# A decoder trunk in split fp32: v projected from the transposed, unscaled x, the MLP's square on ScalarE, and the order of three matmuls

## The chip, the core and the metric

The kernel runs on one core of a Trainium2 chip. The metric is the device time of one execution in microseconds. Of the kernel before there are three timed runs and one profiled execution. TensorE (PE in the profile) multiplies, ScalarE (ACT), VectorE (DVE) and GpSimd (POOL) do the elementwise work, and SyncE (SP) issues nearly all the DMA transfers. Sums of matmuls are gathered in eight PSUM banks of 128 partitions by 512 fp32 numbers.

## The reference

512 tokens of 1024 numbers go through two layers. Layer 0 mixes with a forgetting attention of 16 heads, layer 1 with a short convolution; each mixer is followed by an MLP with a squared ReLU and by a gated embedding.

```python
def rmsnorm(x, g):
    return x * lax.rsqrt(jnp.mean(x * x, -1, keepdims=True) + 1e-6) * g

def fox_attention(h, w_in, b_f, w_out):         # h: 512 x 1024, 16 heads of 64
    proj = h @ w_in                             # q, k, v and 16 forget logits
    ...
    c = lax.cumsum(log_sigmoid(f_logit + b_f))  # over the tokens
    s = q @ k.T / 8 + c[:, None] - c[None, :]   # causal, softmax, times v
    return o @ w_out

def sq_relu_mlp(h, w_up, w_down):               # 1024 -> 4096 -> 1024
    return jnp.square(jax.nn.relu(h @ w_up)) @ w_down

for i in range(2):
    m = fox_attention(rmsnorm(x, g[0]), ...) if i == 0 else short_conv(...)
    x = x + rmsnorm(m, g[1])
    x = x + rmsnorm(sq_relu_mlp(rmsnorm(x, g[2]), ...), g[3])
    x = x + rmsnorm((p[i] @ w_ple_proj[i]) * sigmoid(rmsnorm(x, g[4]) @ w_ple_gate[i]), g[5])
```

## The kernel before, in words

**Numbers.** Each fp32 operand of a matmul is held as a pair of fp32r tiles, a high part and a low part. `split` (L231 to L234) makes a pair: a cast on ScalarE writes the high part, a subtraction on VectorE (for some weights GpSimd) the low part. `mm3` (L223) multiplies two pairs with three matmuls: high by high, low of the first operand by high of the second, high of the first by low of the second. The profile names them L225, L226 and L227. Weights arrive by DMA in one of 14 raw buffers (`raw`) and are split into `wh` and `wl`; `prepare` emits these splits a number of tiles ahead.

**The start.** x is loaded by token blocks of 128 (`xa`, `xc`). The gain of the first norm is spread over the partitions by two matmuls with a row of ones (L883, `g`). For each token block, ScalarE sums squares (`junk`, L256), GpSimd makes the reciprocal root (`n_r_y`), VectorE multiplies x by root and gain (`n_h`, L264), TensorE transposes in eight 128 by 128 pieces (`n_p`, L273), and the result is split into `hTh` and `hTl` by `keep`. From hT the kernel projects v in three column chunks: chunk 0 (272 columns: 256 of v and the 16 forget logits), chunk 1 (512) and chunk 2 (256), each for one token block after the other and all eight k inside a block. `keep_v` splits the sums of v from PSUM into pages (L233 and L234, two pieces of 128 by 128 for each 256 columns). `logs` makes log-sigmoids, `tri` is a triangle of ones (L620), and `sums_of_logs` multiplies them on TensorE (`ps_c`, L388) into the running sum c. c goes to DRAM as `neg_c` and comes back as a bias of the scores. Then come the q and k projections (`qk`), the scores (`sc`), softmax and `ps_o`.

**The MLP.** FF is worked in eight groups. `up` multiplies and hands a bank to a ReLU on ScalarE (`r`, L731), then VectorE squares it (`q`, L717). In the first seven groups the down product is done in seven products on half-size blocks, with sums of blocks of q made on GpSimd (`s`, L745); the pieces of q and their sums are split into `A11h`, `A11l`, `A12h`, `A12l`, `S1h` and so on by `split`. The last group makes the square twice: once on ScalarE straight into the high part (`hh`, L807) and once on VectorE (`q`), so that the low part (`hl`, L810) is the difference. The first group of an MLP is done in two halves of 256 tokens.

**What sets the order.** Inside `manual_schedule` blocks the engines run in program order. Elsewhere a scheduler places the instructions of each engine by its own simulation of the program. Each engine then runs its own queue in order; a DMA queue issues in order, with at most eight transfers of SP's under way. The manual block of the start ends with the splits of v's chunk 0; `tri`, `logs` and what follows are placed by the scheduler.

Of the kernel before, what the change touches and what calls it, by code (L numbers as in the profile page):

```python
# [41 lines left out]
LATE = 0  # L42
PLE_OFF = 34000
# [22 lines left out]
def trunk(ctx: ExitStack, tc, g4T, x, pT, g, wv, wqk, bf, wo, wci, cw, wco, wup, wdn, wpp, wpg, out):  # L66
# [156 lines left out]
    def mm3(ps, a, b, start, stop):  # L223

        nc.tensor.matmul(ps, a.hi, b.hi, start=start, stop=False)  # L225
        nc.tensor.matmul(ps, a.lo, b.hi, start=False, stop=False)  # L226
        nc.tensor.matmul(ps, a.hi, b.lo, start=False, stop=stop)  # L227
        streamed[0] += 3 * ps.shape[-1]
        due()

    def split(hi, lo, src, eng=nc.vector):  # L231

        nc.scalar.copy(hi, src)  # L233
        eng.tensor_tensor(out=lo, in0=src, in1=hi.bitcast(F32), op=ALU.subtract)  # L234

# [82 lines left out]
    def load_x(name, t):  # L318
        xs = [page(f"{name}{t}_{n}") for n in range(2)]
        for n in range(2):  # L320
            eng = nc.scalar if name == "xa" and n else nc.sync
            eng.dma_start(xs[n][:, :S], x[t * P : (t + 1) * P, n * S : (n + 1) * S])
# [30 lines left out]
    def attention(hT, first_x, g0, by_hand):  # L353
# [49 lines left out]
        def values(c, t, soon=SOON, between=None):  # L403

            c0, width = V_CHUNKS[c]
            n_v = min(width, D - c0)
            ps = bank(f"v{c}_{t}")
            for k in range(KT):
                if width == 256:
                    w = wide("v", c, k // 2).at(lambda u: u[:, k % 2 * 256 : k % 2 * 256 + 256])  # L410
                else:
                    w = wide("v", c, k, soon=soon)
                if k == 5 and between:
                    between()
                mm3(ps[:, :width], tokens(hT, k, t), w, k == 0, k == KT - 1)

            def keep_v():
# [12 lines left out]

            return keep_v
# [150 lines left out]
        name = "n0"  # L582
        E, done_v = mybir.EngineType, []
# [410 lines left out]
```

## Time and the profile before

| | us |
|---|---|
| three timed runs | 1247.27, 1247.38, 1251.42 |
| their median | 1247.38 |
| the profiled execution's own time | 1249.03 |
| span of the profile, first to last instruction | 1247.3 |
| TensorE busy | 1222.8 |
| VectorE busy | 909.4 |
| ScalarE busy | 626.1 |
| GpSimd busy | 639.4 |

The granted TensorE clock was 0.997 of full speed over the span. Durations of matmuls overlap in the profile, since the next one starts before the last one's results are out: for how long TensorE is held by a matmul, one reads the distance from its start to the next start. The waits view sums, for each pair of instructions, how long an engine stood still for the other. The timeline lists an engine's instructions with their start, with the idle time ahead of them in brackets.

### The profile page before, as it was taken

The page shows a single profiled execution, that of the slowest core. Times are in us where ns is not written, and L with a number is a line of the kernel's source. Part 1 is how long each engine was busy: PE and PEld are TensorE (multiplying, and loading weights), DVE is VectorE, ACT ScalarE, POOL GpSimd, SP SyncE. Part 2 cuts the span into 40 slices and gives each one's busy share as a digit, 9 for nine tenths or more (in the row PEclk, how much of TensorE's full clock was granted, in tenths as well). Part 3 has the DMA queues.
Part 4 walks back from the last instruction along what each step waited for, and adds up shares of the span by engine and source line. Part 5 has one row for each costly group of instructions (what it writes and reads, how often), then busy time and mean ns, then how long its engine had stood idle before and what let it go on. Part 6 is the DMA issues. An engine that isn't in the chain of part 4 may idle for free.

```text
span 1247.3 us, 17921 instructions
## 1 busy us (share of the span) xinstructions
PE 1222.8 (98%) x5972; PEld 1024.7 (82%) x5972; DVE 909.4 (73%) x1386; ACT 626.1 (50%) x1325; POOL 639.4 (51%) x647
## 2 busy tenths in 40 slices
PE   7999999999999999999999999999999999999997
PEld 5888887788888888887889988889778888888785
DVE  5657787676888878979867444457778898779962
ACT  5467787555544534454655233333654345525541
POOL 2028766147878777875311000017777778778210
PEclk9999999999999999999999999999999999999999
DMA  7455442541343224427513232432422442236401
GB/s 254 150 139 157 127 123 65 160 145 56 123 135 100 77 95 135 128 68 255 142 51 106 75 96 87 162 118 69 127 62 82 136 135 93 68 110 184 137 17 52
DMA packets 82943, 143.45 MB, mean 115 GB/s; under 512 B 9825, under 2 KB 17041, under 8 KB 82849
## 3 DMA queue, kind: packets, MB, share of 16 engines
q1 hardware_dynamic: 82640, 142.03, 37.3%
q8 instruction: 47, 0.77, 0.3%
q14 instruction: 48, 0.39, 0.1%
q10 hardware_dynamic: 144, 0.26, 0.1%
q0 software_dynamic: 64, 0.00, 0.0%
HBM read 135.89 MB, written 6.37 MB: 114 GB/s over the span
## 4 chain that ended last, share of the span: by engine, by line
PE 74%; DVE 10%; POOL 5%; issue 4%; ACT 3%; DMA 3%; SPq 0%; DVEq 0%; POOLq 0%; ACTq 0%
PE dn L226 6%; PE dn L227 5%; PE up L226 5%; PE up L225 5%; PE up L227 5%; PE dn L225 5%; DVE wl L234 5%; POOL s L745 3%; PE pg L227 2%; PE pg L225 2%; PE pg L226 2%; PE qk L225 2%; PE qk L226 2%; PE qk L227 2%; DVE acc L777 2%
## 5 line engine op out<-in xcount | busy, mean ns | idle before, releaser
L234 DVE TENSOR_TENSOR wl<-raw,wh 128x512 fp32r<-128x512 f32 (+1 forms) x372 | 345.8, 979 | 27.0 <-ACT wh L233 26.7
L226 PE MATMUL up<-hTh,wl 128*128 128x512 f32 (+1 forms) x576 | 210.2, 365 | 0.0
L227 PE MATMUL up<-hTl,wh 128*128 128x512 f32 (+1 forms) x576 | 209.7, 366 | 0.0
L225 PE MATMUL up<-hTh,wh 128*128 128x512 f32 (+1 forms) x576 | 209.3, 366 | 0.0
L233 ACT CAST wh<-raw 128x512 fp32r<-128x512 f32 (+1 forms) x372 | 202.1, 619 | 1.9 <-PE ps_o L534 1.6
L234 POOL TENSOR_TENSOR wl<-T,wh 128x512 fp32r<-128x512 f32 x112 | 160.5, 1466 | 35.8 <-ACT wh L233 32.0
L225 PEld LDWEIGHTS up<-hTh,wh 128*128 128x128 f32 x576 | 108.6, 189 | 17.5
L226 PEld LDWEIGHTS up<-hTh,wl 128*128 128x128 f32 x576 | 108.6, 189 | 17.5
L227 PEld LDWEIGHTS up<-hTl,wh 128*128 128x128 f32 x576 | 108.3, 189 | 17.5
L777 DVE TENSOR_TENSOR acc<-dn,acc 128x512 f32<-128x512 f32 x168 | 107.3, 678 | 9.5 <-PE dn L227 9.4
L134 POOL TENSOR_TENSOR T<-raw,raw 128x512 f32<-128x512 f32 x56 | 88.7, 1596 | 36.9 <-DMA raw<-in_wdn 28.9
L731 ACT ACTIVATE r<-up 128x512 f32<-128x512 f32 (+1 forms) x72 | 38.7, 547 | 125.5 <-PE up L227 116.6
L134 POOL TENSOR_TENSOR T<-raw,T 128x512 f32<-128x512 f32 x56 | 91.4, 1632 | 2.2
L717 DVE TENSOR_TENSOR q<-r 128x512 f32<-128x512 f32 (+1 forms) x72 | 68.1, 952 | 29.0 <-ACT r L731 28.9
L248 POOL TENSOR_SCALAR cor_r_v<-cos,cos 128x1 f32<-128x1 f32 x4 | 1.6, 396 | 159.1 <-ACT junk L256 159.1
L233 ACT CAST A11h<-q 128x256 fp32r<-128x256 f32 x28 | 11.4, 406 | 100.7 <-DVE q L717 100.7
L233 ACT CAST wh<-T 128x512 fp32r<-128x512 f32 x112 | 61.2, 617 | 0.0
L784 POOL TENSOR_TENSOR acc<-acc,acc 128x512 f32<-128x512 f32 x28 | 46.9, 1707 | 10.0 <-DVE acc L777 10.0
L225 PE MATMUL qk<-hTh,wh 128*128 128x512 f32 x128 | 50.8, 397 | 0.0
L227 PE MATMUL qk<-hTl,wh 128*128 128x512 f32 x128 | 50.4, 394 | 0.0
L226 PE MATMUL qk<-hTh,wl 128*128 128x512 f32 x128 | 50.4, 393 | 0.0
L225 PE MATMUL pg<-wh,hTh 128*128 128x512 f32 x128 | 50.3, 393 | 0.0
(240 smaller groups left out, 3133.3 us busy)
## 6 DMA issues: line engine op xcount, KB each, us to landing
raw<-in_wup SPq DMA_DIRECT2D x128, 256.0 KB, 2.9
raw<-in_wdn SPq DMA_DIRECT2D x128, 256.0 KB, 2.8
raw<-in_wci SPq DMA_DIRECT2D x48, 256.0 KB, 3.0
raw<-in_wqk SPq DMA_DIRECT2D x32, 256.0 KB, 3.3
raw<-in_wpg SPq DMA_DIRECT2D x32, 256.0 KB, 3.6
g<-in_g SPq DMA_DIRECT2D x18, 256.0 KB, 5.7
prl<-neg_c SPq DMA_DIRECT2D x16, 256.0 KB, 6.6
raw<-in_wo SPq DMA_DIRECT2D x16, 256.0 KB, 2.8
```

Of the source, the lines that this page charges most:

```text
L134: nc.gpsimd.tensor_tensor(out=B[name, p], in0=B[a, p], in1=B[b, p], op=ALU.subtract)
L225: nc.tensor.matmul(ps, a.hi, b.hi, start=start, stop=False)
L226: nc.tensor.matmul(ps, a.lo, b.hi, start=False, stop=False)
L227: nc.tensor.matmul(ps, a.hi, b.lo, start=False, stop=stop)
L233: nc.scalar.copy(hi, src)
L234: eng.tensor_tensor(out=lo, in0=src, in1=hi.bitcast(F32), op=ALU.subtract)
L248: nc.gpsimd.tensor_scalar(out=v, in0=parts[0], scalar1=parts[1], scalar2=EPS, op0=ALU.add, op1=ALU.add)
L717: nc.vector.tensor_tensor(out=out, in0=r, in1=r, op=ALU.mult)
L731: nc.scalar.activation(r[:, :n], ps[:, :n], AF.Relu)
L745: sums = lambda out, a, b, op: nc.gpsimd.tensor_tensor(out=out, in0=a, in1=b, op=op)
L777: nc.vector.tensor_tensor(out=a, in0=banks[s], in1=a, op=ALU.add)
L784: nc.gpsimd.tensor_tensor(out=a, in0=a, in1=acc[i, s][:, :S], op=ALU.add)
```

## The change

The host hands over two more arrays: `xT`, which is x transposed (eight tiles of 128 features by 512 tokens), and `g0T`, the gain of the first norm as a column for each tile. Four things follow.

1. The start no longer transposes. `uT[k]` is xT[k] times its gain, split by `split_by` (ScalarE, then one VectorE instruction); v is projected from uT, and each token's root `r0[t]` is multiplied in when v is split from PSUM. Chunks 0 and 1 now run k outside and the four token blocks inside, so each holds four banks. For q and k, the roots are spread as a row over all partitions by four matmuls (`r_row`), and `normed_tokens(k)` multiplies xT[k] by gain and row (`h`) and splits that into `hTh` and `hTl`. The manual block now reaches to the splits of v's chunk 1 and the first four `normed_tokens`.
2. Before the first projection TensorE does sixteen matmuls of 128 by 128 on a tile of zeros (`warm`, `idle`).
3. `square` in the MLP runs on ScalarE.
4. `mm3` does high by high, high by low, low by high.

```diff
         nc.tensor.matmul(ps, a.hi, b.hi, start=start, stop=False)
-        nc.tensor.matmul(ps, a.lo, b.hi, start=False, stop=False)
-        nc.tensor.matmul(ps, a.hi, b.lo, start=False, stop=stop)
+        nc.tensor.matmul(ps, a.hi, b.lo, start=False, stop=False)
+        nc.tensor.matmul(ps, a.lo, b.hi, start=False, stop=stop)
...
+    def split_by(hi, lo, src, by):
+
+        nc.scalar.mul(hi, src, by)
+        nc.vector.scalar_tensor_tensor(
+            out=lo, in0=src, scalar=by, in1=hi.bitcast(F32), op0=ALU.mult, op1=ALU.subtract
+        )
...
-        vs = [[page(f"v{t}_{i}", F32R) for i in range(4)] for t in range(NB)]
+        vs = [{} for _ in range(NB)]
...
-        def values(c, t, soon=SOON, between=None):
+        def keep_v(c, t, ps):
...
             n_v = min(width, D - c0)
+            if n_v < width:
+                nc.vector.scalar_tensor_tensor(
+                    out=logit[:, t * H : (t + 1) * H], in0=ps[:, n_v:width], scalar=r0[t],
+                    in1=b_f, op0=ALU.mult, op1=ALU.add,
+                )
+            for c1 in range(0, n_v, 256):
+                src = ps[:, c1 : c1 + 256].rearrange("p (h d) -> p h d", d=HD)
+                b = (c0 + c1) // 256
+                vs[t][b] = page(f"v{t}_{b}", F32R)
+                block = vs[t][b].rearrange("p (h r) -> p h r", r=P)
+                split_by(block[:, :, :HD], block[:, :, HD:], src, r0[t])
+
+        def values(c, t):
+
-                if n_v < width:
-                    nc.vector.tensor_tensor(
-                        out=logit[:, t * H : (t + 1) * H], in0=ps[:, n_v:width], in1=b_f,
-                        op=ALU.add,
-                    )
-                for c1 in range(0, n_v, 256):
-                    src = ps[:, c1 : c1 + 256].rearrange("p (i e d) -> p i e d", e=2, d=HD)
-                    block = vs[t][(c0 + c1) // 256].rearrange("p (i r) -> p i r", i=2)
-                    for e in range(2):
-                        hi = block[:, :, 192 * e : 192 * e + HD]
-                        lo = block[:, :, 64 + 64 * e : 128 + 64 * e]
-                        split(hi, lo, src[:, :, e, :])
-
-            return keep_v
+                w = wide("v", c, k // 2).at(lambda u: u[:, k % 2 * 256 : k % 2 * 256 + 256])
+                mm3(ps[:, :256], tokens_of(uT[k], t), w, k == 0, k == KT - 1)
+            keep_v(c, t, ps)
...
-        def rows(t):
-            r = stats(t, first_x[t], name)
-            return [scaled(t, n, first_x[t], r, g0, name) for n in range(2)]
-
-        def turn_rows(t, hs):
-            for n in range(2):
-                keep(t, n, turned(t, n, hs[n], name), hT)
+        E = mybir.EngineType
+        r0, uT = {}, []
+        r_row, every = page("r_row"), page("every")
+        nc.gpsimd.memset(every[:, :P], 1.0)
+
+        def chunk(c, after):
+
+            width = V_CHUNKS[c][1]
+            banks = [bank(f"v{c}_{t}") for t in range(NB)]
+            for k in range(KT):
+                if c == 0:
+                    uT.append(Pair(page(f"uTh{k}", F32R), page(f"uTl{k}", F32R)))
+                    split_by(uT[k].hi[:, :S], uT[k].lo[:, :S], first_xT[k][:, :S], g0_col[:, k : k + 1])
+                w = wide("v", c, k, soon=0)
+                for t in range(NB):
+                    mm3(banks[t][:, :width], tokens_of(uT[k], t), w, k == 0, k == KT - 1)
+                after(k)
+            return banks
...
         with tc.manual_schedule(engines={E.PE, E.DVE, E.Activation}):
-            r = stats(0, first_x[0], name)
-            prepare(3)
-            hs = {0: [scaled(0, n, first_x[0], r, g0, name) for n in range(2)]}
-            prepare(4)
-            for n in range(2):
-                keep(0, n, turned(0, n, hs[0][n], name), hT)
-                prepare(5 + n)
-            prepare(KT)
-            hs[1] = rows(1)
-            hs[2] = rows(2)
+            banks = {0: chunk(0, lambda k: None)}
+
+            def between(k):
+                t = k - 1
+                if 0 <= t < NB:
+                    r0[t] = stats(t, first_x[t], "n0")
+                    nc.gpsimd.tensor_scalar(
+                        out=every[:, (t + 1) * P : (t + 2) * P] if t < NB - 1 else diag[:, :P],
+                        in0=ident, scalar1=r0[t], scalar2=None, op0=ALU.mult,
+                    )
+                if k >= NB:
+                    keep_v(0, k - NB, banks[0][k - NB])
+                    prepare(where["v", 2, 0] + 1 + k - NB)
+
+                if k == KT - 2:
+                    spread = bank("r_row")
+                    for t in range(NB):
+                        nc.tensor.matmul(
+                            spread[:, t * P : (t + 1) * P], every[:, :P],
+                            every[:, (t + 1) * P : (t + 2) * P] if t < NB - 1 else diag[:, :P],
+                            start=True, stop=True,
+                        )
+                    nc.scalar.copy(r_row[:, :S], spread)
+
+            def normed_tokens(k):
+                h = page(f"h0_{k}")
+                nc.vector.scalar_tensor_tensor(
+                    out=h[:, :S], in0=first_xT[k][:, :S], scalar=g0_col[:, k : k + 1],
+                    in1=r_row[:, :S], op0=ALU.mult, op1=ALU.mult,
+                )
+                split(hT.hi[:, k, :], hT.lo[:, k, :], h[:, :S])
+
+            diag = page("diag")
+            banks[1] = chunk(1, between)
+            prepare(where["qk", 0, 0] + 2)
             for t in range(NB):
-                between = (lambda: turn_rows(t + 1, hs[t + 1])) if t + 1 < NB else None
-                done_v.append(values(0, t, 0, between))
-                if t + 3 < NB:
-                    hs[t + 3] = rows(t + 3)
-                if t:
-                    prepare(KT + 3 * t)
-                    done_v.pop(0)()
-        done_v.pop(0)()
+                keep_v(1, t, banks[1][t])
+                normed_tokens(t)
         tri = page("tri", F32R)
         ones = page("ones")
...
         nc.vector.tensor_copy(tri[:, :S], ones[:, :S])
         logs()
         for t in range(NB):
-            values(1, t)()
-            if t == 2:
+            values(2, t)
+            normed_tokens(NB + t)
+            if t == 1:
                 sums_of_logs(tri)
         bias(0)
         bias(1)
-        for t in range(NB):
-            values(2, t)()
...
         def square(out, r):
-            nc.vector.tensor_tensor(out=out, in0=r, in1=r, op=ALU.mult)
+            nc.scalar.activation(out, r, AF.Square)
...
+        nc.scalar.dma_start(g0_col, g0T)
+        for k in range(KT):
+            (nc.scalar if k < 2 else nc.sync).dma_start(first_xT[k][:, :S], xT[k])
+            fetch(k + 1)
+        first_x = []
+        for t in range(NB):
+            fetch(KT + t + 1)
+            first_x.append(load_x("xc", t))
+    idle = bank("idle")
+    for _ in range(WARM):
+        nc.tensor.matmul(idle[:, :P], warm[:, :P], warm[:, :P], start=True, stop=True)
```

The order of the instructions moves at three places. The first is VectorE's queue in the start, around the making of `tri`. Before, it stood among the small steps of the logs (`f_u`, `f_r`, `f_ru`), after the last split of v's chunk 0 (`v_3`):

```order
L369 TENSOR_SCALAR f_u<-f_e 128x64
L234 TENSOR_TENSOR v_3_147<-v_3_412,v_3_147 128x2x64
L372 SCALAR_TENSOR_TENSOR f_r<-f_u,f_e 128x64
L620 CAST tri<-ones 128x512
L375 RECIPROCAL f_ru<-f_u 128x64
```

Now it stands behind the splits of chunk 1 of all four token blocks and behind four `normed_tokens`; these are the last rows of that chain, for token block 3 and k of 3, with the preceding block's end:

```order
L629 SCALAR_TENSOR_TENSOR h_2_602<-xT_90,g_col,r_row 128x512
L235 TENSOR_TENSOR hTl<-h_2_602,hTh 128x512
L240 SCALAR_TENSOR_TENSOR v_0_606<-v_3_345,n_r_y,v_0_606 128x4x64
L240 SCALAR_TENSOR_TENSOR v_1_609<-v_3_345,n_r_y,v_1_609 128x4x64
L629 SCALAR_TENSOR_TENSOR h_3_612<-xT_91,g_col,r_row 128x512
L648 CAST tri<-ones 128x512
L235 TENSOR_TENSOR hTl<-h_3_612,hTh 128x512
```

The splits of v wait for ScalarE and, through it, for TensorE, and `hTl` waits for ScalarE's `hTh`. `tri` needs only GpSimd's triangle of ones, but it is made after them, since the queue runs in order.

The second place is TensorE's queue where it uses `tri`. Before, `ps_c` followed the third token block of v's chunk 1 (512 columns):

```order
L225 MATMUL v_2_598<-wh_443,hTh 128x512
L226 MATMUL v_2_598<-wh_443,hTl 128x512
L227 MATMUL v_2_598<-wl_444,hTh 128x512
L388 MATMUL ps_c<-tri,lf_h 16x512
L388 MATMUL ps_c<-tri,lf_l 16x512
L388 MATMUL ps_c<-tri,lf_h 16x384
```

Now it follows the second token block of chunk 2 (256 columns), and the other two token blocks of chunk 2 come behind it:

```order
L226 MATMUL v_1_709<-wh_558,uTh_321 128x256
L227 MATMUL v_1_709<-wl_559,uTh_321 128x256
L228 MATMUL v_1_709<-wh_558,uTl_322 128x256
L395 MATMUL ps_c<-tri,lf_h 16x512
L395 MATMUL ps_c<-tri,lf_l 16x512
L395 MATMUL ps_c<-tri,lf_h 16x384
```

The first row of `ps_c` waits for the cast of `tri` on VectorE, and all of TensorE's work behind it waits with it.

The third place is ScalarE's queue in the first group of the MLP (names carry layer, group, f and half). Before, ReLUs stood next to each other and the squares on VectorE:

```order
L731 ACTIVATE r_0_0_256_3931<-up_0_0_256_3906 128x256
L731 ACTIVATE r_0_1_256_3961<-up_0_1_256_3936 128x256
L233 CAST A12h_0_1_3964<-q_0_1_3691 128x512
L233 CAST S1h_0_1_3972<-s_0_1_3968 128x512
L233 CAST S3h_0_1_3976<-s_0_0_3934 128x512
```

Now each ReLU is followed by its square, and what VectorE held of these rows is gone there:

```order
L758 ACTIVATE r_0_0_256_3932<-up_0_0_256_3907 128x256
L744 ACTIVATE q_0_0_3691<-r_0_0_256_3932 128x256
L758 ACTIVATE r_0_1_256_3962<-up_0_1_256_3937 128x256
L744 ACTIVATE q_0_1_3692<-r_0_1_256_3962 128x256
L234 CAST A12h_0_1_3965<-q_0_1_3692 128x512
L234 CAST S1h_0_1_3973<-s_0_1_3969 128x512
L234 CAST S3h_0_1_3977<-s_0_0_3935 128x512
```

Here `A12h` needs the square on its own engine alone, where before it waited for another engine; the casts behind it keep their order.

More of the change, by code (lines that the diff above doesn't have):

```diff
@@ L42 @@
 LATE = 0
+WARM = 16
 PLE_OFF = 34000
@@ L65, in trunk @@
 @with_exitstack
-def trunk(ctx: ExitStack, tc, g4T, x, pT, g, wv, wqk, bf, wo, wci, cw, wco, wup, wdn, wpp, wpg, out):
+def trunk(ctx: ExitStack, tc, g4T, x, xT, pT, g, g0T, wv, wqk, bf, wo, wci, cw, wco, wup, wdn, wpp, wpg, out):
     nc = tc.nc
@@ L320, in load_x @@
         for n in range(2):
-            eng = nc.scalar if name == "xa" and n else nc.sync
-            eng.dma_start(xs[n][:, :S], x[t * P : (t + 1) * P, n * S : (n + 1) * S])
+            nc.sync.dma_start(xs[n][:, :S], x[t * P : (t + 1) * P, n * S : (n + 1) * S])
         return xs
@@ L351, in mixer_out, with attention @@
                 then(t)
-    def attention(hT, first_x, g0, by_hand):
+    def attention(hT, first_xT, g0_col, first_x, by_hand):
         b_f = consts.tile([P, H], F32, tag="bf", name="b_f")
-        vs = [[page(f"v{t}_{i}", F32R) for i in range(4)] for t in range(NB)]
+        vs = [{} for _ in range(NB)]
         n_f = NB * H
@@ L867, in ple @@
                 then(t)
-    one = page("one")
-    nc.vector.memset(one[:1, :P], 1.0)
-    rows = [page(f"row{n}") for n in range(2)]
-    for n in range(2):
-        nc.gpsimd.dma_start(rows[n][:1, :], g[0:1, n * S : (n + 1) * S])
-    with tc.manual_schedule(engines={mybir.EngineType.SP, mybir.EngineType.Activation}):
-        first_x = [load_x("xa", 0)]
-        fetch(4)
-        first_x.append(load_x("xc", 1))
-        fetch(KT)
-        first_x += [load_x("xc", t) for t in (2, 3)]
-    g0 = [bank(f"g0_{n}") for n in range(2)]
-    for n in range(2):
-        nc.tensor.matmul(g0[n], one[:1, :P], rows[n][:1, :], start=True, stop=True)
+    g0_col = consts.tile([P, KT], F32, tag="g0_col", name="g0_col")
+    warm = page("warm")
+    nc.vector.memset(warm[:, :S], 0.0)
+    first_xT = [page(f"xT{k}") for k in range(KT)]
+    with tc.manual_schedule(engines={mybir.EngineType.SP, mybir.EngineType.Activation}):
+        nc.scalar.dma_start(g0_col, g0T)
[9 more added lines that the diff above has]
+        nc.tensor.matmul(idle[:, :P], warm[:, :P], warm[:, :P], start=True, stop=True)
     kept = dram.tile([2, NB, 2, P, S], F32, tag="kept", name="kept")
@@ L886, in trunk @@
     by_hand = ExitStack()
-    lhs, opened = attention(hT, first_x, g0, by_hand)
+    lhs, opened = attention(hT, first_xT, g0_col, first_x, by_hand)
     oT = lhs
```

12 lines of the change are left out of this document (2 added, 10 removed).

## The prediction, on record before the kernel ran

> **What bounds the kernel now.** First the page's busy times, and GpSimd's busy tenths in forty slices of 31 us:
>
> ```profile
> PE 1222.8 (98%) x5972; PEld 1024.7 (82%) x5972; DVE 909.4 (73%) x1386; ACT 626.1 (50%) x1325; POOL 639.4 (51%) x647
> POOL 2028766147878777875311000017777778778210
> ```
>
> TensorE bounds it: time can only come from where TensorE stands still, runs at half clock, or does work that goes. The waits view of TensorE names the standstills (us in total, times, longest):
>
> ```profile
> PE g L883 <- DMA row<-in_g: 6.3, 1, 6.3
> PE dn L226 <- DVE hl L810: 2.5, 2, 1.3
> PE dn L226 <- DVE A12l L234: 0.5, 2, 0.3
> ```
>
> The first is the start, the others are the MLP's. A standstill shorter than a matmul's pipeline is in no wait, so I also count matmuls by stretch at the beginning of each MLP (stretch, length, busy and count, clock, DMA):
>
> ```profile
> 291.65:306.00 14.35, 13.82 (x55) 1.00 0.01 2
> 868.00:883.00 15.00, 14.47 (x60) 1.00 0.00 0
> ```
>
> The distance of two matmuls of 512 columns is 0.23 us (below). 55 of them fill 12.65 of 14.35 us and 60 fill 13.8 of 15.0, so 1.7 and 1.2 are lost there: 2.9 together.
>
> **The front, before.** TensorE's timeline up to the first q and k matmul:
>
> ```profile
> 6.35 3.75 PE L883 MATMUL g<-row,one 1*128 1x512 f32 x4 [6.35 <-DMA row<-in_g]
> 11.81 0.59 PE L225 MATMUL v<-wh,hTh 128*128 128x272 f32 x1
> 13.16 0.43 PE L225 MATMUL v<-wh,hTh 128*128 128x272 f32 x1
> 14.52 0.41 PE L225 MATMUL v<-wh,hTh 128*128 128x272 f32 x1
> 33.07 0.29 PE L225 MATMUL v<-wh,hTh 128*128 128x272 f32 x1
> 35.21 0.29 PE L227 MATMUL v<-wl,hTh 128*128 128x272 f32 x1
> 46.89 0.40 PE L388 MATMUL ps_c<-tri,lf_h 128*16 128x512 f32 x1
> 48.06 0.44 PE L225 MATMUL v<-wh,hTh 128*128 128x512 f32 x1
> 53.59 0.28 PE L225 MATMUL v<-wh,hTh 128*128 128x256 f32 x1
> 65.10 0.40 PE L225 MATMUL qk<-hTh,wh 128*128 128x512 f32 x1
> ```
>
> Distances: the six from 13.16 to 14.52 are 0.227 each, the seventeen from 33.07 to 35.21 are 0.126, so the start ran at half clock until about 14.6. The 24 matmuls of 512 columns from 48.06 to 53.59 are 0.23 each, the 96 of 256 from there to 65.10 are 0.12, and `ps_c` took 1.17. **65.10 is the mark** against which the new front is laid.
>
> **The front, after.** The prices of its steps, from the DMA view (KB, us to landing), the timeline, the groups between 20 and 65 us and of the page (busy, mean ns), and one tile's durations (min/median/max ns):
>
> ```profile
> xa<-in_x ACTq DMA_DIRECT2D x1, 256.0 KB, 4.1
> 7.08 1.36 ACT L233 CAST wh<-raw 128x272 fp32r<-128x272 f32 x4
> 7.51 1.15 DVE L234 TENSOR_TENSOR wl<-raw,wh 128x272 fp32r<-128x272 f32 x3 [6.47 <-ACT wh L233]
> L370 ACT ACT_TABLE_LOAD x1 | 1.3, 1283 | 0.0
> L233 ACT CAST wh<-raw 128x512 fp32r<-128x512 f32 x20 | 11.0, 624 | 0.0
> L264 DVE SCALAR_TENSOR_TENSOR n_h<-xc,n_r_y,g 128x512 f32<-128x512 f32 x2 | 1.4, 744 | 1.1 <-POOL n_r_y L251 1.1
> L234 DVE TENSOR_TENSOR hTl<-n_p,hTh 128x512 fp32r<-128x512 f32 x5 | 3.3, 685 | 0.3 <-ACT hTh L233 0.2
> L233 ACT CAST hTh<-n_p 128x512 fp32r<-128x512 f32 x4 | 2.2, 594 | 1.9 <-PE n_p L273 1.9
> L233 ACT CAST A11h<-q 128x256 fp32r<-128x256 f32 x28 | 11.4, 406 | 100.7 <-DVE q L717 100.7
> L234 DVE TENSOR_TENSOR A11l<-q,A11h x28: 424/826/969, 286.7 to 1115.6; 128x256 fp32r<-128x256 f32 x28
> L234 DVE TENSOR_TENSOR v<-v,v 128x128 fp32r<-128x128 f32 x30 | 8.2, 287 | 11.3 <-ACT v L233 11.0
> L620 DVE CAST tri<-ones 128x512 fp32r<-128x512 f32 x1 | 0.4, 418 | 0.0
> ```
>
> *Start.* xT's first tile is issued on ScalarE's queue behind the gain column, some 1.2 us in, and lands 4.1 later, at 5.3. A table load waits for the same transfer: 6.6. Then `uTh` 0.6, `wh` 0.34, beside that `uTl` (priced as `n_h`) 0.74, and `wl` 0.38: TensorE runs from about 8.4, against 11.81. Eight transfers under way with 4.1 us each bring one k (two transfers) per 1.0 us, ScalarE needs 0.95 and VectorE 1.1 for a k, TensorE 12 × 0.126 = 1.5, so TensorE sets the pace. 96 matmuls of 272 columns: 8.4 + 12.1 = 20.5. 84 of 512: + 19.3 = 39.8. For `r_row`, `g` was two plain fp32 matmuls of 512 columns at half clock, 3.75 in all: one of 128 columns at full clock is 0.235, four are 0.9: 40.7. Twelve of 512, 2.8: 43.5. 48 of 256, 5.8: **TensorE stands before `ps_c` at 49.3.** Gone are the transposes, the gain's matmuls and their wait, and the half-clock start.
>
> *`tri`.* On VectorE `tri` now stands behind the splits of chunk 1 and four `normed_tokens`. ScalarE copies `r_row` until 41.4, splits the last piece of chunk 0 until 41.8, casts three weights (0.62 each, less a little since they overlap) until 43.5, and makes chunk 1's first high part by 43.9. Then each token block costs VectorE 0.42, a wait of 0.41 for ScalarE's second piece, 0.42, `h` 0.74, a wait of 0.59 for `hTh`, and `hTl` 0.69; with 0.15 for handing over, 3.4 us. A split of v with a factor, from PSUM, in pieces of 4 by 64, is in no row. I take the shortest 128 by 256 split, 0.42, as nearest in size; the ends are 0.29 (the 128 by 128 row) with ScalarE's second piece ready, a block of 2.75, and 0.83 (the median beside GpSimd). Three blocks are 10.2, the fourth up to `h` 2.0, `tri` 0.42: 43.9 + 12.6 = 56.5. **TensorE waits 7.2 us**, more than the 6.3 of the old start. Then `ps_c` 1.2 and 48 of 256, 5.8: 63.5.
>
> *Half clock after the wait.* The timeline in the attention shows what a stop brings:
>
> ```profile
> 198.31 0.50 PE L534 MATMUL ps_o<-ph,v 128*128 128x512 f32 x1 [1.06 <-ACT ph L233]
> 199.11 0.62 PE L493 MATMUL sc<-kh,q 128*128 128x512 f32 x1
> 202.51 0.41 PE L225 MATMUL o<-wh,hTh 128*128 128x512 f32 x1
> ```
>
> The eight distances there are 0.425 instead of 0.23: 1.6 us. So the first q and k matmul comes at 65.1, and **the front gives 0.0**. Its low end (the block of 2.75) has `tri` at 53.9, 2.6 better, or 4.2 if the half clock goes with it; its high end stands below as a rival.
>
> The Trainium skill, page "TensorE: Matmul & The Clock Gate", Part 1 (the HAM clock gate), says that an idle window of some 3.4 us brings half clock and some 3.4 us of sustained work full clock again. By that a stop of 7 us is certain to cost 1.7, where the sum has 1.6. The trace agrees on the way back (199.11 to 202.51 is 3.4) but not on the way down, where the longest stop was 1.06.
>
> *Behind the front.* The running sum now ends about nine us later, and VectorE has weights and `h` to do ahead of it, so `neg_c` goes out some 16 us later. Before, its last bias was ready at 65.6, and the scores began at 81.4:
>
> ```profile
> 65.34 0.29 POOL L480 TENSOR_SCALAR_AFFINE_SELECT prl<-prl 128x128 f32<-128x128 f32 x1 [0.60 <-PE v L227]
> 81.44 0.28 PE L493 MATMUL sc<-kh,q 128*128 128x256 f32 x1
> ```
>
> That slack covers it almost exactly; I cost it at nothing, and at up to 2 us if that cover is gone.
>
> **The MLP.** With the square on ScalarE, `A11h` (100.7 us of waiting for VectorE in its row) follows its square on the same engine. Where TensorE does not wait this is worth nothing. ScalarE is busy half of the span, and 72 more squares of about 0.6 fit. What does wait:
>
> ```profile
> 581.32 0.63 ACT L807 ACTIVATE hh<-r 128x512 fp32r<-128x512 f32 x1
> 583.14 0.84 PE L225 MATMUL dn<-wh,hh 128*128 128x512 f32 x3
> 583.64 0.68 DVE L717 TENSOR_TENSOR q<-r 128x512 f32<-128x512 f32 x1
> 293.99 0.62 ACT L233 CAST A12h<-q 128x512 fp32r<-128x512 f32 x1 [2.30 <-DVE q L717]
> 293.76 0.80 POOL L745 TENSOR_TENSOR s<-q 128x256 f32<-128x256 f32 x1 [0.76 <-DVE q L717]
> 294.66 1.19 PE L225 MATMUL dn<-wh,A12h 128*128 128x512 f32 x4
> ```
>
> *Last group, twice.* On ScalarE the square follows `hh` and is done by 582.6, so `hl` starts when VectorE is free at 583.64 and ends by 584.35 (0.69, as `hTl`). TensorE does three `wh·hh` from 583.14 and, in the new order, `wl·hh` next; it asks for `hl` at about 584.3. Of the 2.5 in the waits I take 2.3. *`A12l`, twice:* 0.5 in the waits and about as much in pipelines that drain; 0.8. *The beginnings, twice:* ScalarE had its last ReLU at 291.69 and waited 2.30 for VectorE's squares. On its own queue the last square takes 0.41, and `A12h` is there at 292.7 instead of 294.6. What is late next are GpSimd's sums: four of 0.8 from 292.1, then `S1h` at 0.62, 295.9, while TensorE asks for it after twelve matmuls on `A12`, not before 297. Of the 2.9 I take 2.8, since a first wait of a pipeline may stay.
>
> The new order of three matmuls asks for each `wl` one matmul earlier. Weights are split many tiles ahead, so it costs nothing; without that cover, as at the very first k, 0.23 each.
>
> **Sum.** 0.0 + 2.3 + 0.8 + 2.8 = 5.9. The profiled execution took 1249.03, so 1243.1 by it; it stands 1.65 above the median, and against the median 1247.38 − 5.9 = **1241.5 us**.
>
> **The rivals.** *VectorE's chain is short* (blocks of 2.75): 1241.5 − 2.6 = 1238.9. For it: v's present pieces take VectorE 0.287. Against: in the same row it waited 11.0 for ScalarE. Chance 0.14. *It is long, and the kernel slower.* Beside GpSimd the split's median was twice its shortest; with 0.83 for it and `h` and `hTl` doubled, a block takes 5.5, `tri` comes 8.2 later, 1249.7. It decides from a block of 5.0. Against: GpSimd's slice from 31 to 62 us shows 0. Chance 0.08. *The sums stay last.* If GpSimd's sums or their splits end after TensorE asks, the beginnings give nothing: 1244.3. For it: a sum of 0.80 can be slower beside VectorE, and the margin is 1.1. Chance 0.15. *The warm-up warms nothing.* `g` and the transposes kept TensorE at work from 6.35 to 11.81, and the clock was half until 14.6. If zeros do no more, the sixteen take 0.47 each, until about 8.9, and 16 of v's matmuls run at half: 0.5 + 1.6 = 2.1 later, 1243.6. Chance 0.13. By the Trainium skill's section above the warm-up would do, since it lasts beyond 3.4 us; the trace so far speaks against it with those 5.5 us.
>
> **Chances and range.** My case keeps 0.50. The range 1236.5 to 1247.5 takes in the short chain with its half clock spared (1237.3) and, above, sums that stay last with a late `neg_c` (1246.3) and a little of the warm-up; it leaves out the long chain. What a measurement can tell from no change is about 0.5%: faster is below 1241.1, slower above 1253.6. My case lies on the first line, so half of it is faster; with the short chain, 0.40. Slower is half of the long chain, 0.04; the rest is same.
>
> **What would show it.** Right: a wait of `ps_c` for `tri` of 6 to 8 us near 49, matmuls of 256 at 0.24 behind it, the first q and k matmul near 65, no wait for `hl`, and `A12h` without a gap ahead of it. Wrong: that wait under 4 us or over 10; v's first matmuls at 0.22; a wait for `S1h` at the beginning of an MLP; or a new wait of TensorE in the attention, where `neg_c` is short of time.

## The result

The changed kernel took 1239.3 us (median of 4 runs, 1238.79 to 1239.58), the kernel before 1247.65 beside it. The ratio is 0.9926, with a 95% interval of 0.9906 to 0.9945: 8.35 us less by the medians, and 9.4 by the spans of the two profiles, 1247.3 and 1237.9. The forecast was 1241.5 with a range of 1236.5 to 1247.5.

The waits view of TensorE after the change (us in total, times, longest):

```profile
PE ps_c L395 <- DVE tri L648: 7.9, 1, 7.9
PE ps_o L535 <- ACT ph L234: 1.7, 2, 1.2
PE idle L912 <- DVE warm L899: 1.5, 1, 1.5
```

The waits for `g` and `hl` are gone, and the largest wait is the new one, `ps_c` for `tri`. `A12l` is not in this view either, but in that of a second profile of the same kernel it stands with 0.6 us, about what it had before. TensorE's timeline of the front:

```profile
8.01 0.39 PE L226 MATMUL v<-wh,uTh 128*128 128x272 f32 x1 [0.32 <-ACT wh L234]
8.84 0.39 PE L227 MATMUL v<-wl,uTh 128*128 128x272 f32 x1 [0.44 <-DVE wl L235]
49.19 0.28 PE L228 MATMUL v<-wh,uTl 128*128 128x256 f32 x1
57.35 0.59 PE L395 MATMUL ps_c<-tri,lf_h 128*16 128x512 f32 x1 [7.88 <-DVE tri L648]
59.44 0.52 PE L226 MATMUL v<-wh,uTh 128*128 128x256 f32 x1
65.97 0.40 PE L226 MATMUL qk<-hTh,wh 128*128 128x512 f32 x1
```

The last matmul ahead of `ps_c` starts at 49.19, the next one 8.2 us later; `ps_c` takes 2.09 us instead of 1.17, so the clock is half there. The first q and k matmul comes at 65.97, against 65.10 before. The front did not gain: it lost 0.9 in this profile, and 0.1 in the second one (65.19). There the first tile of xT landed 0.5 us earlier, and half clock after the wait held for four matmuls of v instead of seven.

To see where the 9.4 us are, I take the starts of four stages from the timelines. Before:

```profile
265.45 0.28 PE L225 MATMUL up<-hTh,wh 128*128 128x256 f32 x1
604.56 0.39 PE L225 MATMUL pp<-wh,wh 128*128 128x512 f32 x1
843.12 0.28 PE L225 MATMUL up<-hTh,wh 128*128 128x256 f32 x1
1181.56 0.39 PE L225 MATMUL pp<-wh,wh 128*128 128x512 f32 x1
```

And after:

```profile
264.70 0.52 PE L226 MATMUL up<-hTh,wh 128*128 128x256 f32 x3
599.51 0.39 PE L226 MATMUL pp<-wh,wh 128*128 128x512 f32 x1
838.00 0.52 PE L226 MATMUL up<-hTh,wh 128*128 128x256 f32 x3
1171.96 0.39 PE L226 MATMUL pp<-wh,wh 128*128 128x512 f32 x1
```

`up` begins an MLP and `pp` follows it. The distance between two such rows is what a stage took:

| stage | before | after | difference |
|---|---|---|---|
| front, to the first q and k matmul | 65.10 | 65.97 | +0.87 |
| attention, to the first `up` | 200.35 | 198.73 | -1.62 |
| first MLP | 339.11 | 334.81 | -4.30 |
| gated embedding, convolution | 238.56 | 238.49 | -0.07 |
| second MLP | 338.44 | 333.96 | -4.48 |
| from there to the end | 65.76 | 65.89 | +0.13 |

Of the gain 8.8 us are the MLPs'. The attention's 1.6 stand against the 0.9 that the front lost.

### The profile page after: what moved, and what is told of

It reads as the page before. It is cut to its first block, busy times and chain, and to the rows that moved or that the text cites. A ratio compares the mean times of both kernels' runs of the same rounds, so it can differ in the third digit from the quotient of the medians.

```text
span 1237.9 us, 17975 instructions
## 1 busy us (share of the span) xinstructions
PE 1215.2 (98%) x5976; PEld 1027.0 (83%) x5976; DVE 859.1 (69%) x1306; ACT 674.9 (55%) x1390; POOL 643.7 (52%) x650
## 4 chain that ended last, share of the span: by engine, by line
PE 94%; DVE 2%; ACT 1%; issue 1%; DMA 1%; POOL 0%; POOLq 0%; DVEq 0%; ACTq 0%; SPq 0%
PE up L228 9%; PE up L227 9%; PE up L226 9%; PE dn L228 8%; PE dn L226 8%; PE dn L227 8%; PE qk L226 2%; PE qk L227 2%; PE pg L228 2%; PE pg L226 2%; PE pg L227 2%; PE qk L228 2%; PE sc L494 1%; PE o L227 1%; PE pT L513 1%; PE b L228 1%
## 5 line engine op out<-in xcount | busy, mean ns | idle before, releaser
L235 POOL TENSOR_TENSOR wl<-T,wh 128x512 fp32r<-128x512 f32 x112 | 156.7, 1430 | 32.6 <-ACT wh L234 31.3
L235 DVE TENSOR_TENSOR A12l<-q,A12h 128x512 fp32r<-128x512 f32 x28 | 26.4, 944 | 43.9 <-ACT A12h L234 43.9
L235 DVE TENSOR_TENSOR A11l<-q,A11h 128x256 fp32r<-128x256 f32 x28 | 26.4, 944 | 40.7 <-ACT A11h L234 40.7
L811 POOL TENSOR_TENSOR acc<-acc,acc 128x512 f32<-128x512 f32 x28 | 47.0, 1710 | 10.1 <-DVE acc L804 10.1
```

What stands on the lines that cost most here:

```text
L811: nc.gpsimd.tensor_tensor(out=a, in0=a, in1=acc[i, s][:, :S], op=ALU.add)
```

## The experiments

Each was run beside the kernel before on the same chip; medians of the kernel before were 1248.3 to 1248.8 there. The changed kernel was run again among them (the last experiment).

**tri early.** The lines that make `tri` and `ones` go ahead of the manual block of the start.

```diff
+        tri = page("tri", F32R)
+        ones = page("ones")
...
+        nc.vector.tensor_copy(tri[:, :S], ones[:, :S])
         with tc.manual_schedule(engines={E.PE, E.DVE, E.Activation}):
             banks = {0: chunk(0, lambda k: None)}
```

> The changed kernel with tri made ahead of the start's manual block, so that it is the first thing VectorE does and no longer stands behind the splits of v and four normed_tokens. Theory (the wait of ps_c for tri is what ate the gain of the front): ps_c starts within 1 us of the last matmul ahead of it, near 49.5, there is no half clock behind it, and the first q and k matmul comes near 56. From there VectorE, which does weights and h first, lets TensorE wait 3 to 5 us for hTl of k 4 to 7, so the first projection ends some 5 us earlier than in the changed kernel: about 1234.5 us. Rival (the attention behind it is set by ScalarE's and VectorE's chain of softmax, so time won ahead of it comes back as waits between 190 and 235 us): the first q and k matmul near 56 all the same, but less than 1.5 us in the total, 1238 to 1239.5.

1237.78 us, ratio to before 0.9915 (0.990 to 0.9931); span 1235.1. The wait of `ps_c` is gone and the first q and k matmul comes 10.1 us earlier than in the changed kernel's first profile. Then TensorE's timeline has:

```profile
55.90 0.40 PE L226 MATMUL qk<-hTh,wh 128*128 128x512 f32 x1
...
72.02 0.39 PE L228 MATMUL qk<-hTh,wl 128*128 128x512 f32 x1
75.04 0.36 PE L494 MATMUL sc<-kh,q 128*128 128x256 f32 x1 [2.63 <-DVE q L456]
75.23 0.28 PE L494 MATMUL sc<-kl,q 128*128 128x256 f32 x1
76.79 0.58 PE L494 MATMUL sc<-kh,q 128*128 128x256 f32 x1 [1.28 <-DVE q L456]
77.17 0.41 PE L494 MATMUL sc<-kl,q 128*128 128x256 f32 x1
77.39 0.63 PE L226 MATMUL qk<-hTh,wh 128*128 128x512 f32 x1
```

There is no wait for `hTl` between 55.90 and 72.02, but two for q ahead of the scores, 3.9 us, and behind them matmuls of 512 columns 0.42 apart: the granted clock was half from 75.6 to 82.5, with TensorE at work for 5.7 us of it, which costs about 2.8. Of the 10.1 us, 2.5 were left at the first `up` (262.20 against 264.70), and 1.5 by the medians. So the theory's first half held (the wait for `tri` had eaten the gain), its second half had the wrong place, and the rival's place, the end of the attention, was wrong too: the loss lies ahead of 83 us.

**The short chain.** The same instructions in another order, still with `tri` behind them.

```diff
             for t in range(NB):
-                keep_v(1, t, banks[1][t])
-                normed_tokens(t)
+                h = page(f"h0_{t}")
+                nc.vector.scalar_tensor_tensor(
+                    out=h[:, :S], in0=first_xT[t][:, :S], scalar=g0_col[:, t : t + 1],
+                    in1=r_row[:, :S], op0=ALU.mult, op1=ALU.mult,
+                )
+                for b in range(2):
...
+                    split_by(block[:, :, :HD], block[:, :, HD:], src, r0[t])
+                    if b == 0:
+                        split(hT.hi[:, t, :], hT.lo[:, t, :], h[:, :S])
```

> The changed kernel with another order in the chain ahead of tri: for each token block VectorE makes h first, ScalarE puts hTh between its two pieces of v, and hTl stands between VectorE's two pieces. The same instructions, but neither engine has to stand still for the other: a block takes 2.3 to 2.5 us instead of 3.45. Theory (the length of this chain is what ps_c waits for, one for one): tri comes 3 to 4 us earlier, the wait of ps_c falls from 7.9 to 4 or 5 us, and the total falls by the same 3 to 4 us, to about 1235.8. Rival (what follows is bound elsewhere, the weights, h and neg_c behind the chain): the wait falls as said, but a new wait ahead of the scores takes it back, and the total stays within 1 us of the changed kernel, 1239.

1236.05 us, ratio 0.9903 (0.9888 to 0.9918); span 1235.7. VectorE's chain in the changed kernel, one token block:

```profile
47.80 0.48 DVE L240 SCALAR_TENSOR_TENSOR v<-v,n_r_y,v 128x256 fp32r<-128x256 f32 x1
48.82 0.48 DVE L240 SCALAR_TENSOR_TENSOR v<-v,n_r_y,v 128x256 fp32r<-128x256 f32 x1 [0.54 <-ACT v L239]
49.22 0.74 DVE L629 SCALAR_TENSOR_TENSOR h<-xT,g_col,r_row 128x512 f32<-128x512 f32 x1
50.64 0.69 DVE L235 TENSOR_TENSOR hTl<-h,hTh 128x512 fp32r<-128x512 f32 x1 [0.68 <-ACT hTh L234]
51.25 0.48 DVE L240 SCALAR_TENSOR_TENSOR v<-v,n_r_y,v 128x256 fp32r<-128x256 f32 x1
```

From 47.80 to 51.25 are 3.45 us, of which 1.22 are spent waiting for ScalarE. In the short chain the same distance is 2.43 (45.62 to 48.05). Its waits view, then TensorE's timeline:

```profile
PE ps_c L395 <- DVE tri L658: 5.2, 1, 5.2
```

```profile
63.25 0.40 PE L226 MATMUL qk<-hTh,wh 128*128 128x512 f32 x1
```

The wait falls by 2.7. The first q and k matmul comes 2.7 earlier than in the first profile of the changed kernel (1.9 than in the second), and the total fell by 3.25. The cast of `tri` ended 3.5 us earlier; the wait fell by less, since TensorE also stood there 0.8 earlier. The wait for `tri` follows the chain's length.

**Both, and TensorE's order.** Both edits together:

> tri early, as in the first experiment, and the short chain together. With tri early alone the first q and k matmul came at 55.9 instead of 66.0, but TensorE then waited 4.2 us for q ahead of the scores, ran at half clock for 2.5 us more, and 2.6 us were left. Theory (VectorE's queue between 43 and 75 us is now the bound: what it does 3 to 4 us earlier comes out at the scores): the wait for q falls below 2 us, the half clock goes with it, and the total is 3 to 6 us under tri early alone, 1230 to 1233. Rival (the place of the scores is set by the order the scheduler made for TensorE, not by VectorE): within 1 us of tri early alone, 1236.

1237.38 us, ratio 0.9913 (0.9898 to 0.9927). The wait for q stood unchanged, so the length of VectorE's chain was not what set it:

```profile
PE sc L494 <- DVE q L456: 3.9, 2, 2.6
```

In both kernels with an early `tri` the scheduler had dealt the 24 matmuls of the second pair's first half among those of the first pair. The first pair's sums were then finished only two matmuls ahead of the scores, and q after them. So the order was written out:

```diff
+            together = {s: bank(f"qk{i}_{s}") for s in (1, 0)} if i == 0 else {}
+            for k in range(KT) if i == 0 else ():
+                for s in (1, 0):
+                    mm3(
+                        together[s], narrow("qk", i, k=k, c=s * P),
+                        hT.at(lambda h: h[:, k, :]), k == 0, k == KT - 1,
+                    )
...
+        with tc.manual_schedule(engines={E.PE}):
             for _ in project(0):
                 pass
             main = stream()
             for _ in range(8):
                 next(main)
```

> tri early and the short chain, with TensorE's order written out for the first projections: both halves of the first pair of heads, k by k, then the next pair, then the scores. With tri early the scheduler had put the second pair's first half between the two halves of the first, so q was finished just ahead of the scores and TensorE waited 3.9 us for VectorE's q, with half clock behind it. Theory (that order is what the gain of an early tri was lost to): no wait for q, the first scores at 72 to 73 instead of 74.8, no half clock at 77, and the total 4 to 6 us under both without this order, 1231 to 1233. Rival (VectorE is the bound, hTl of k 6 and 7 or the bias come as late as before): a wait for hTl or for the bias takes its place, and the total stays at 1235 to 1237.

> tri early and the written order of the first projections, with the chain as in the changed kernel, 3.5 us longer. Theory (with the order mended, VectorE's chain is next): TensorE waits 3 to 4 us for hTl of k 5 to 7 near 66, the total is 1 to 4 us over the kernel that has the short chain too, 1234 to 1236. Rival (the chain is not needed any more): within 1 us of it.

With the short chain 1232.88 us (1230.81 to 1234.3), ratio 0.987 (0.9853 to 0.9886); without it 1233.56, ratio 0.9884 (0.9865 to 0.9903). Their waits, first with the short chain, then without:

```profile
PE sc L501 <- DVE q L463: 1.1, 1, 1.1
...
PE qk L227 <- DVE hTl L235: 0.8, 1, 0.8
```

```profile
PE qk L227 <- DVE hTl L235: 1.5, 1, 1.5
...
PE qk L226 <- ACT hTh L234: 0.6, 1, 0.6
```

The order was what the early `tri` had lost a good part of its gain to: the first `up` now comes at 258.76 and 259.03, 5.9 and 5.7 us ahead of the changed kernel's first profile, instead of 2.5. Some 4 of the 10 us still do not arrive there. **This version beats both kernels, by some 16 us the one before and 6 the changed one.**

By the medians the second expectation's theory missed: the chain is worth 0.7 us once the order is mended. The profiles make that less firm. With the long chain the two waits for hT, 2.1 us together, were followed by half clock from 64.9 to 68.3, and the scores began at 76.55; with the short chain they began at 73.26. Of these 3.3 us the wait for q took 1.1, and half clock at 192.2 to 195.6, in the trace of the short chain alone, took 1.6. That second dip is not the chain's doing (see the attention below), so what the chain is worth stays open between 0.7 and some 2 us.

**The square alone, the order alone.** The kernel before with one edit each: the square on ScalarE, or the order of the three matmuls.

> The kernel before with one edit, the square on ScalarE. Theory (the square's place is what TensorE waited for in the MLPs; between the two traces the MLPs gave 8.8 us): 7 to 9 us faster than before, about 1239.5, with no wait for hl or A12h left. Rival (part of it is the low part that now comes third, above all for hl and A12l): 4 to 6 us faster, about 1242.5, with waits for hl and A12l left in the waits view.

> The kernel before with one edit, the order of the three matmuls. Theory: a matmul that comes one place later forgives 0.23 us for each of the waits for hl and A12l and nothing elsewhere: 0 to 1 us faster, about 1247. Rival (the order is worth as much as the square): 2 to 4 us faster, about 1244.5.

The square alone: 1241.78 us, ratio 0.9949 (0.9934 to 0.9964); its MLPs took 335.47 and 334.61 between the same rows, 7.5 less than before. By the medians it gave 6.5, between the two forecasts; the waits are as the theory had them. No wait for `hl` or `A12` is in its view, but one for `S1l` of 0.8. The order alone: 1251.86, ratio 1.003 (1.002 to 1.0041), slower than before, which neither theory had. Its waits:

```profile
PE dn L227 <- DVE hl L810: 4.1, 2, 2.4
...
PE dn L225 <- ACT r L731: 1.1, 2, 0.5
```

`hl` was waited for 1.6 us longer than before, though it is asked for one matmul later, and in the second MLP half clock followed that wait from 1162.3 to 1165.7, another 1.6. The wait for `A12l` is gone. This trace is of the shortest run, 1249.78; why the median is 2 us above it, and what made `hl` later, was not tried.

**The changed kernel without its new order, and without both MLP edits.**

> The changed kernel with the three matmuls in their old order alone. The square alone left 0.9 us more standing still at A12 of each MLP than the changed kernel has, and the order alone made the kernel before 3 us slower. Theory (with the square on ScalarE the low part third is worth what is left at A12l, and no more): 1 to 1.5 us slower than the changed kernel, 1240.5. Rival (the order costs here as it did before): 2 to 3 us faster than the changed kernel, 1236.5.

> The changed kernel with the square back on VectorE and the three matmuls back in their old order, so that only the start is changed. Theory (the start gives nothing, the MLP everything): the MLPs' 8.8 us come back, 1247 to 1248.5, the same as before. Rival (the front was worth something that the MLP's part hid): 2 us or more under before, 1245.

The old order: 1241.23 us, ratio 0.9947 (0.993 to 0.9964), so the new one is worth some 1.9 by the medians where the square is on ScalarE; the MLPs of this profile took 336.40 and 335.56, 3.2 more than in the changed kernel's first profile and 2.6 more than in its second. Its waits show what the new order shortens:

```profile
PE dn L227 <- DVE A12l L235: 1.9, 2, 0.9
```

The start alone: 1251.21, ratio 1.0014 (1.0002 to 1.0027), no gain at all, and by the medians 2.7 us more than the kernel before, which neither theory had. The runs spread from 1247.16 to 1252.55, the longer ones at a granted clock of 0.991 to 0.994 instead of 0.995; the profiled one took 1248.04, so its trace does not show what the longer ones lost. Its waits have the old ones back beside the new one:

```profile
PE ps_c L395 <- DVE tri L648: 7.9, 1, 7.9
PE dn L227 <- DVE hl L837: 3.0, 2, 1.8
```

**The warm-up.** Once without the sixteen matmuls (`WARM = 0`), once with them on a single partition:

```diff
-        nc.tensor.matmul(idle[:, :P], warm[:, :P], warm[:, :P], start=True, stop=True)
+        nc.tensor.matmul(idle[:, :P], warm[:1, :P], warm[:1, :P], start=True, stop=True)
```

> The changed kernel without the sixteen matmuls on zeros. Theory (they lifted the clock: v's first matmuls lie 0.126 apart in the changed kernel): the first 13 to 16 of v's matmuls at 0.227, the wait of ps_c shifted by the same amount, since VectorE's chain hangs on v, and the kernel 1.5 us slower than the changed one, about 1240.8. Rival (time lost before ps_c is hidden in the wait there): within 0.4 us of the changed kernel, 1239.3.

> The changed kernel with the sixteen matmuls on one partition of the zeros instead of 128, as the gain's matmuls of the kernel before had one. Theory (work on one row does not lift the clock, which is why the kernel before was at half clock until 14.6 in spite of 5.5 us of work): the sixteen take as long as before, the clock is still half when v begins, v's first 16 to 20 matmuls lie 0.227 apart, and the start is 1.5 to 2.2 us later, as without any warm-up: 1241 to 1242. Rival (any matmul lifts it): v's matmuls 0.126 apart from the second on, 1239.3.

Without them 1242.33 us, ratio 0.9951 (0.9936 to 0.9966); on one partition 1242.15, ratio 0.9948 (0.9936 to 0.9959): 3 us over the changed kernel, more than expected. TensorE's timeline of the second:

```profile
1.50 7.19 PE L912 MATMUL idle<-warm 1*128 1x128 f32 x32 [1.50 <-DVE warm L899]
8.62 0.59 PE L226 MATMUL v<-wh,uTh 128*128 128x272 f32 x1
9.02 0.43 PE L227 MATMUL v<-wl,uTh 128*128 128x272 f32 x1
...
13.55 0.38 PE L226 MATMUL v<-wh,uTh 128*128 128x272 f32 x1
13.77 0.29 PE L227 MATMUL v<-wl,uTh 128*128 128x272 f32 x1
```

TensorE was busy from 1.50, and the clock was still half until 13.6: twenty distances of 0.227, 2.1 us lost. Without any warm-up as many were lost, from 8.2 to 13.0. The wait of `ps_c` was 7.9 in both, so none of this hid in it. The first q and k matmul came at 68.15 (without) and 68.90 (one partition), 2.2 and 2.9 after the changed kernel's first profile. Some 0.8 of each is a longer half clock after `ps_c`. In the totals of these two traces half clock after the stops near 200 comes on top, which the changed kernel's two traces do not have.

**The changed kernel again.**

> The changed kernel once more, unaltered, beside the others on the same chip. Theory (the 1.6 us that the attention gave between the two traces came from the clock, not from the change: both had the same stops near 197, but only before did half clock follow): the total within 1.5 us of 1239.3; the stops of 0.7 and 1.2 us are there again, while half clock after them may or may not be. Rival (the change removed the cause of the half clock there): no half clock near 200 again, as in the first trace of this kernel.

1239.31 us, ratio 0.9924 (0.9909 to 0.9939). Its attention took 198.75, and again no half clock followed the stops near 197. This alone would speak for the rival. Against it: the start alone and the order alone had none either, while the square alone had it as before. Below it is taken up once more.

## Why the prediction was right, and where it was not

**The front, right.** TensorE was to stand before `ps_c` at 49.3 and did at 49.5. A token block on VectorE was to take 3.4 us and took 3.45, with 0.48 for the split with a factor that I had priced at 0.42. `tri` was to be ready at 56.5; its cast ran from 56.79 to 57.20, and the wait was 7.9 against 7.2. Of these 0.7, 0.4 are low parts of weights (`wl`) that VectorE had to finish ahead of the chain, so that the first split began at 44.34 and not at 43.9; I had counted their casts on ScalarE alone. Half clock after the wait was priced at 1.6: from `ps_c` to the first q and k matmul are 8.62 and 8.32 us in the two profiles, against 6.97 with an early `tri` and the full clock, so it cost 1.65 and 1.35. The first q and k matmul was to come at 65.1 and came at 65.97 and, in the second profile, 65.19. The experiments with an early `tri` and a short chain show that this wait is the cause, and the start alone that no gain is left.

**The step that was mis-sized: the MLP.** The terms were 2.3 for the last groups, 0.8 for `A12l` and 2.8 for the beginnings, 5.9 together; 8.8 was measured. The mechanism held for the beginnings and the last groups, and in part for `A12l`: the wait for `hl` is gone, and `A12h` is ready ahead of TensorE:

```profile
289.85 0.42 ACT L744 ACTIVATE q<-r 128x256 f32<-128x256 f32 x1
290.30 0.62 ACT L234 CAST A12h<-q 128x512 fp32r<-128x512 f32 x1
```

```profile
293.66 0.39 PE L226 MATMUL dn<-wh,A12h 128*128 128x512 f32 x1
```

The size of the beginnings came from counting records by stretch. A record counts in a stretch that it only touches, and three records of the second stretch had 256 columns: 53 matmuls of 512 columns began in the first, not 55, and in the second 54 of 512 and three of 256, not 60 of 512. At 0.2275 each, 2.3 us were lost in each stretch, 4.6 instead of 2.9. The distances from start to start give all three terms, summed over both MLPs wherever a distance is more than 0.03 us above that (transposes left out): the beginnings lost 4.6 before and 0.4 after, 4.1 gained where I took 2.8; the last groups 3.2 and 0.2, 3.0 where I took 2.3; the second group, with `A12l`, 1.6 and 0.6 (1.2 in the second profile), 1.0 or 0.4 where I took 0.8. The other 0.6 or so is spread thinly. Behind each wait one more matmul whose pipeline had drained lies some 0.1 further apart, which the waits view does not sum. The squares were also earlier than I had them, at 289.85 and not 292, since the ReLUs no longer queue behind a cast that waits: before, `A11h` at 290.45 had waited 1.10 for VectorE's square, with the last three ReLUs behind it. By the medians the total missed by 2.2, the terms of the MLP by 2.9.

**What I had at nothing: the attention.** It gave 1.6 us between the two traces, the half clock at 199.1 to 202.5 before. After the change the same stop is followed by the full clock:

```profile
199.17 0.50 PE L535 MATMUL ps_o<-ph,v 128*128 128x512 f32 x1 [1.19 <-ACT ph L234]
199.51 0.39 PE L494 MATMUL sc<-kh,q 128*128 128x512 f32 x1
```

In the fourteen profiles of this study the two waits for `ph` stand there each time, 1.6 to 1.7 us together, and half clock followed them in eight. It follows in the kernel before and with the square alone, not with the start alone or the order alone, so none of the edits alone decides it. Both profiles of the changed kernel are without it.

The granted clock in the traces shows what decides. In each of the fourteen it changes only at distances that are whole multiples of 3.41 us, on a grid whose place in the program differs from execution to execution. What counts is how much TensorE does between two edges of it. Stretches between edges, first of the kernel before (two), then of the changed kernel (stretch, length, TensorE busy and count, granted clock, DMA):

```profile
195.69:199.10 3.41, 2.17 (x9) 1.00 0.33 103
199.10:202.52 3.42, 3.42 (x10) 0.50 0.02 6
```

```profile
197.60:201.02 3.42, 2.23 (x10) 1.00 0.16 63
```

Busy time looks alike, but counted in columns, as a share of what a whole stretch takes at full clock, the first has 0.37: it holds the sparse work ahead of the longer stop and the stop itself, and ends 0.8 us behind it. In the changed kernel the edge at 197.60 parts the sparse work from the stop, and dense matmuls fill the rest behind it: the stretches on its two sides have 0.50 and 0.54. Among all stretches at full clock in the fourteen traces, the 33 that half clock followed have 0.37 or less, and the others 0.40 or more. With the changed kernel's very stops, 0.5 and 1.2 us, half clock did follow in the short chain and without the warm-up, whose stretches there have 0.30. So the 1.6 us are an accident of where the grid fell, and the change did not earn them.

**The rivals.** The warm-up did warm (v's matmuls 0.126 apart from 9 us on, the clock full from 6.5). I had doubted it because the gain's matmuls and the transposes had not lifted the clock; the run on one partition shows that the gain's matmuls, with one row, were no work to it. The sums did not stay last, and VectorE's chain was neither short nor long. `neg_c` was in time: the scores began 16.35 us after the first q and k matmul, as before (16.34).

## What to carry to other kernels

A gain ahead of a point where engines meet is worth what the last to arrive leaves of it: here the 9 us by which the start was shorter (first q and k matmul at 55.90 with an early `tri`, 65.10 before) ended in a wait for a 0.42 us cast that needed nothing late and stood in the wrong place of its queue. Look in the order of every engine for such small instructions behind long chains; and where one is moved, look again, since the next wait may be made by the scheduler's answer to it. When idle time is counted by stretch, count the instructions that start in it, by shape. Where a stop is followed by half clock in one trace and not in another, look at more than one execution before either is put down to the change.

## What the runs showed of the hardware

Work on one partition did not lift TensorE's clock: sixteen matmuls on 128 partitions of zeros did while they lasted (6.19 us; v's matmuls after them lie 0.126 apart), the same on one partition for 7.2 us did not, and v's then ran at 0.227 for 4.5 us more. The Trainium skill, page "TensorE: Matmul & The Clock Gate", Part 1 (the HAM clock gate), gives the time of sustained work as some 3.4 us. The traces agree roughly with that for full rows: in the nine profiles with the full warm-up the clock was full 2.9 to 5.9 us after its first matmul. The one on a single partition shows that not all work counts.

After a wait of 5 to 8 us at `ps_c` the clock was half each time, for `ps_c` itself and 4 to 17 matmuls of 256 columns. After the two waits for `ph` it was half in eight profiles of fourteen. The same page says that the window of activity runs free of the program. The traces agree: the changes lie on the grid of 3.41 us above, and in the two profiles of the changed kernel, one program, half clock after `ps_c` lasts from 54.24 to 61.07 and from 53.10 to 59.93, while `ps_c` begins at 57.35 and 56.87.

The share that separates, between 0.37 and 0.40 of a stretch's columns, is worked out from these traces alone: a matmul is taken to hold TensorE for 0.2275 us for each 512 columns, a plain fp32 one (transposes and warm-up, 0.11 us for 128 columns) for twice that, and for double at half clock. Coming back, the 19 stretches that ended half clock have 0.41 or more, the 14 that did not 0.41 or less. A stop much shorter than a stretch can thus bring half clock where the rest of the stretch is thinly filled: the one of 1.06 us did.
